# Ten of twelve pairs of merge-gate products by seven half-width products each

## The chip, the cores and the metric

The kernel runs on one core of one Trainium2 chip. Five engines matter here: TensorE (PE in the profile, its weight loads PEld), VectorE (DVE), ScalarE (ACT), GpSimd (POOL) and the DMA queues that SyncE (SP) and POOL issue to. The metric is the device time of one execution, in microseconds.

## The reference

One layer of a decoder trunk on x of 512 rows by 1024 features, all float32:

```python
h = rmsnorm(x, norm_g)
u = h @ w_in                       # split into a_x, a_z, b_q ... c_z, gate_logits
ya = pool_mixer(a_x) * silu(a_z)
yb = swa_attention(b_q, b_k, b_v, sinks) * silu(b_z)
yc = moba_attention(c_q, c_k, c_v) * silu(c_z)
ga, gb, gc = split(sigmoid(gate_logits), 3)          # each 512 x 1024
merged = ga * (ya @ w_proj_a) + gb * (yb @ w_proj_b) + gc * (yc @ w_proj_c)
out = rmsnorm(x + merged @ w_out, final_norm_g)
```

gate_logits is h (512 x 1024) times 1024 x 3072, the largest product of the layer. ya, yb and yc are 512 x 512 each.

## The kernel before

**Split precision.** Each float32 operand is kept as two float32r parts, hi (a cast on ACT, L103 for weights) and lo (value minus hi on DVE, L104). Each product is three matmuls into one PSUM bank: hi by hi, hi by lo, lo by hi (`mm3`, L125 to L128). In the trace these are the lines L126, L127, L128.

**Layout.** Activations are transposed: features on the 128 partitions, the 512 rows of x along the free axis. h is eight tiles `hT[k]` of 128 x 512, each as hi and lo. A weight block `wr` is 128 x 1024: for an output block of 128 features, the eight 128 x 128 stationary tiles of the contraction. The host packs the blocks; `weight_blocks` (L48) lists them in the order of use.

**Weights.** SP loads the raw block (`load_upto`, L91, 512 KB each, a ring of 4 buffers `wr`). `split_upto` (L106) casts it to `wh` on ACT and forms `wl` on DVE, two blocks ahead of its use (rings of 3), and then asks for the load of the fourth block ahead.

**Two stages.** Until 250.4 us of the span the input projections and the two attentions run, interleaved by a table `todo` that is keyed by matmul chunk (`at`, `tick`). The change leaves that order nearly as it was. Then comes the gate stage. It runs over the eight output blocks j of 128 features: gate a (24 matmuls of 512 columns, L534 to L543, its sigmoid on ACT), the output projection of the block before (`project_out`, L578, eight groups of three matmuls, each added to `acc` by DVE on L585), gate b, gate c, and `project` (L550): three times 12 matmuls of 512 columns, each multiplied by its sigmoid and summed on DVE (L565, L568, L569), the sum split to hi and lo (`merged[j]`). The last three blocks of w_out are left to the end, where they accumulate in PSUM (`tail_mm`, L613) while the final norm runs; its last group is cut into two of 256 columns. In every engine's queue the instructions stand in program order; a matmul waits only for its operands and its bank.

**PSUM.** Four tags of two banks: `big` (gates), `T` (projections), `S` and `PV` (output projections in this stage).

**x for the residual.** Four DMAs of 512 KB on POOL's queue (L517) fill `acc` at the start of the gate stage.

Of the kernel before, what the change touches and what calls it, by code (L numbers as in the profile page):

```python
# [46 lines left out]

def weight_blocks():  # L48

    blocks = [(u, 1024) for u in UNITS]  # L50
    late = []
    for j in range(KT):
        blocks.append((("ga", j), 1024))
        if late:
            blocks.append((("wo", late.pop()), 1024))
        blocks += [(("gb", j), 1024), (("gc", j), 1024), (("pab", j), 1024), (("pc", j), 512)]
        if j < KT - TAIL:
            late.append(j)
    blocks += [(("wo", j), 1024) for j in range(KT - TAIL, KT)]
    return blocks  # L60
# [3 lines left out]
def trunk(ctx: ExitStack, tc: tile.TileContext, a, out: bass.AP):  # L64
# [17 lines left out]
    blocks = weight_blocks()  # L82
    index = {name: n for n, (name, _) in enumerate(blocks)}
# [3 lines left out]
    def raw_tile(n):  # L87
        raw_w[n] = pool.tile([P, 1024], F32, name=f"wr{n}", tag="wr", bufs=4)
        return raw_w[n]

    def load_upto(n):  # L91
        while done["load"] <= min(n, len(blocks) - 1):
            m = done["load"]
            cols = blocks[m][1]
            nc.sync.dma_start(raw_tile(m)[:, :cols], a["w"][m][:, :cols])
# [10 lines left out]
    def split_upto(n):  # L106
        while done["split"] <= min(n, len(blocks) - 1):
# [11 lines left out]
    def split(src, name, two=None):  # L119
        hi, lo = (t2(F32R, name + "h"), t2(F32R, name + "l")) if two is None else (two[:, 0, :], two[:, 1, :])  # L120
        nc.scalar.copy(hi, src)
        nc.vector.tensor_sub(lo, src, hi.bitcast(F32))
        return hi, lo

    def mm3(ps, lh, ll, rh, rl, start, stop):  # L125
        nc.tensor.matmul(ps, lh, rh, start=start, stop=False)  # L126
        nc.tensor.matmul(ps, lh, rl, start=False, stop=False)  # L127
        nc.tensor.matmul(ps, ll, rh, start=False, stop=stop)  # L128
# [17 lines left out]
    xT = [t2(F32, f"xT{k}") for k in range(KT)]  # L146
# [10 lines left out]
    xn = pool.tile([P, NT, D], F32, name="xn", tag="v", bufs=1, padded_shape=[P, 5, 1024])  # L157
    for t in range(NT):
        nc.sync.dma_start(xn[:, t, :], a["x"][t * P:(t + 1) * P, :])
# [27 lines left out]
    for k in range(KT):  # L187
        hi, lo = t2(F32R, f"xgh{k}"), t2(F32R, f"xgl{k}")
# [57 lines left out]
    vt = []  # L246

    def evacuate(u, ps):
# [5 lines left out]
        if kind in ("cq", "ck", "bq", "bk"):  # L254
            hi, lo = split(ps, f"{kind}{i}")
            top, low = slice(0, HD), slice(HD, P)
            if kind[1] == "q":
                two = parts[u] = pair(F32R, f"{kind}{i}two")
                moves = ((two, top, 0, hi, top), (two, low, 0, lo, top),
                         (two, low, 1, hi, low), (two, top, 1, lo, low))  # L260
            else:
                his, los = parts[u] = pair(F32R, f"{kind}{i}his"), pair(F32R, f"{kind}{i}los")
# [4 lines left out]
        elif kind == "cz":  # L267
            full[u] = t2(F32, f"{kind}{i}")
# [5 lines left out]
        else:  # L274
            full[u] = t2(F32, f"{kind}{i}")
# [16 lines left out]
    def turn_v(u):  # L292
# [26 lines left out]

    def pool_mix(i):  # L320
        if not pw:
            pw_raw = t2(F32, "pw_raw")
            nc.gpsimd.dma_start(pw_raw, a["pool_w"])
            pw.extend(split(pw_raw, "pw"))
# [3 lines left out]
        full["oa", i] = t2(F32, f"oa{i}")  # L328
        nc.scalar.activation(full["oa", i], ps, AF.Copy, scale=psc_sb[:, i:i + 1])
# [10 lines left out]
    def head(s):  # L340
        if s not in heads:
# [6 lines left out]
            h.v = n if h.moba else 8 + h.par  # L348
# [43 lines left out]
    def turn(s, b):  # L392
# [19 lines left out]
        hi, lo = t2(F32R, f"pth{s}_{b}"), t2(F32R, f"ptl{s}_{b}")  # L412
# [11 lines left out]
    def weigh(s, half):  # L424
# [15 lines left out]
        if half == 1:  # L440
            kind = "oc" if h.moba else "ob"
            if h.par == 0:
                full[kind, h.block] = t2(F32, f"{kind}{h.block}")
# [19 lines left out]
    for k in range(KT):  # L463
        at(32 + 3 + 5 * k, normed, k)
        at(32 + 5 + 5 * k, normed_rest, k)
    for u in UNITS:
# [48 lines left out]
    acc = pool.tile([P, NT, D], F32, name="acc", tag="v", bufs=1, padded_shape=[P, 5, 1024])  # L515
# [239 lines left out]
```

## Time and profile before

| what | value |
|---|---|
| time, median of 3 runs | 507.12 us (506.67 to 507.14) |
| profiled execution, its own time | 506.78 us |
| its span | 505.0 us |
| mean granted TensorE clock | 0.994 |
| busy: PE / PEld / DVE / ACT / POOL | 494.8 / 402.7 / 305.1 / 232.4 / 33.3 us |
| gate stage, start to last matmul's start | 250.41 to 496.16 us |
| HBM read / written | 47.98 / 2.10 MB |

The profile is one execution. The span runs from the first to the last recorded instruction; the time of the execution is 1.78 us more. Busy times are sums of instructions; matmuls overlap one another, so the pace of TensorE is read from the starts of matmuls that follow one another, not from the length of one. PEld are weight loads, which run beside matmuls. "Idle before <- releaser" names what ended the wait of an engine.

### The profile page before, as it was taken

The page shows a single profiled execution, that of the slowest core. Times are in us where ns is not written, and L with a number is a line of the kernel's source. Part 1 is how long each engine was busy: PE and PEld are TensorE (multiplying, and loading weights), DVE is VectorE, ACT ScalarE, POOL GpSimd, SP SyncE. Part 2 cuts the span into 40 slices and gives each one's busy share as a digit, 9 for nine tenths or more (in the row PEclk, how much of TensorE's full clock was granted, in tenths as well). Part 3 has the DMA queues.
Part 4 walks back from the last instruction along what each step waited for, and adds up shares of the span by engine and source line. Part 5 has one row for each costly group of instructions (what it writes and reads, how often), then busy time and mean ns, then how long its engine had stood idle before and what let it go on. Part 6 is the DMA issues. An engine that isn't in the chain of part 4 may idle for free.

```text
span 505.0 us, 6455 instructions
## 1 busy us (share of the span) xinstructions
PE 494.8 (98%) x2297; PEld 402.7 (80%) x2297; DVE 305.1 (60%) x605; ACT 232.4 (46%) x452; POOL 33.3 (7%) x72
## 2 busy tenths in 40 slices
PE   8999999999999999999999999999999999999993
PEld 5788888888888888888888887888888888888882
DVE  5558877676788975558556626455272563433376
ACT  6655665656565675559464223132222222323344
POOL 2052000000021100000100000000000000000022
PEclk9999999999999999999999999999999999999997
DMA  8999427743622122210552231313232321313004
GB/s 258 398 257 242 147 74 179 197 125 92 174 72 104 43 83 85 83 56 29 199 182 80 85 123 64 125 65 123 85 104 85 102 85 64 125 64 125 0 2 167
DMA packets 22368, 59.94 MB, mean 119 GB/s; under 512 B 3200, under 2 KB 4224, under 8 KB 22336
## 3 DMA queue, kind: packets, MB, share of 16 engines
q1 hardware_dynamic: 21312, 56.63, 35.6%
q0 software_dynamic: 880, 2.89, 1.6%
q8 instruction: 18, 0.29, 0.2%
q14 instruction: 14, 0.11, 0.1%
q10 hardware_dynamic: 144, 0.00, 0.0%
HBM read 47.98 MB, written 2.10 MB: 99 GB/s over the span
## 4 chain that ended last, share of the span: by engine, by line
PE 95%; DVE 2%; ACT 1%; DMA 1%; issue 0%; SPq 0%; ACTq 0%
PE ps_o L438 3%; PE ps_gc L126 3%; PE ps_gb L126 3%; PE ps_gc L127 3%; PE ps_ga L128 3%; PE ps_gb L127 3%; PE ps_gc L128 3%; PE ps_gb L128 3%; PE ps_ga L127 3%; PE ps_ga L126 3%; PE ps_t L410 3%; PE ps_y L126 2%; PE ps_y L128 2%; PE ps_y L127 2%; PE ps_s L369 2%; PE ps_s L368 2%
## 5 line engine op out<-in xcount | busy, mean ns | idle before, releaser
L103 ACT CAST wh<-wr 128x1024 fp32r<-128x1024 f32 (+2 forms) x88 | 83.5, 952 | 166.5 <-PE ps_gc L127 35.7
L104 DVE TENSOR_TENSOR wl<-wr,wh 128x1024 fp32r<-128x1024 f32 (+2 forms) x84 | 91.6, 1095 | 94.1 <-ACT wh L103 93.7
L377 ACT ACTIVATE p<-p,st 128x128 f32<-128x128 f32 (+2 forms) x64 | 33.4, 523 | 34.5 <-DVE st L375 34.4
L585 DVE TENSOR_TENSOR acc<-acc,ps_y 128x512 f32<-128x512 f32 x40 | 24.8, 684 | 15.7 <-PE ps_y L128 15.7
L421 DVE TENSOR_TENSOR ptl<-ps_t,pth 128x512 fp32r<-128x512 f32 (+3 forms) x56 | 26.5, 476 | 7.3 <-ACT pth L420 6.8
L420 ACT CAST pth<-ps_t 128x512 fp32r<-128x512 f32 (+3 forms) x56 | 23.4, 418 | 12.8 <-PE ps_t L410 7.7
L128 PE MATMUL ps_ga<-hh,wl 128*128 128x512 f32 x64 | 25.3, 395 | 0.0
L127 PE MATMUL ps_ga<-hl,wh 128*128 128x512 f32 x64 | 25.3, 395 | 0.0
L128 PE MATMUL ps_gb<-hh,wl 128*128 128x512 f32 x64 | 25.3, 395 | 0.0
L126 PE MATMUL ps_gc<-hh,wh 128*128 128x512 f32 x64 | 25.3, 395 | 0.0
L127 PE MATMUL ps_gc<-hl,wh 128*128 128x512 f32 x64 | 25.3, 395 | 0.0
L128 PE MATMUL ps_gc<-hh,wl 128*128 128x512 f32 x64 | 25.3, 395 | 0.0
L126 PE MATMUL ps_gb<-hh,wh 128*128 128x512 f32 x64 | 25.3, 395 | 0.0
L127 PE MATMUL ps_gb<-hl,wh 128*128 128x512 f32 x64 | 25.3, 395 | 0.0
L126 PE MATMUL ps_ga<-hh,wh 128*128 128x512 f32 x64 | 25.3, 395 | 0.0
L637 POOL TENSOR_TENSOR yo<-acc,fg 128x512 f32<-128x512 f32 x5 | 6.4, 1294 | 241.7 <-DVE acc L627 239.4
L410 PE MATMUL ps_t<-ident,p 128*128 128x128 f32 x136 | 21.3, 272 | 0.0
L390 DVE TENSOR_SCALAR p<-p,st 128x128 f32<-128x128 f32 (+2 forms) x64 | 19.9, 358 | 0.5
L410 PEld LDWEIGHTS ps_t<-ident,p 128*128 128x128 f32 x136 | 16.7, 141 | 3.7
L438 PE MATMUL ps_o<-pth,vt 128*128 128x256 f32 (+1 forms) x64 | 17.8, 296 | 0.0
L438 PE MATMUL ps_o<-ptl,vt 128*128 128x256 f32 (+1 forms) x64 | 17.7, 300 | 0.0
L375 DVE CUSTOM_DVE_ANT_0 p<-ps_s,mask_c,nscale 128x128 f32<-128x128 f32 (+3 forms) x32 | 16.5, 545 | 1.7 <-PE ps_s L369 1.6
(390 smaller groups left out, 1263.4 us busy)
## 6 DMA issues: line engine op xcount, KB each, us to landing
wr<-in_w SPq DMA_DIRECT2D x72, 512.0 KB, 3.3
xT<-in_xT SPq DMA_DIRECT2D x8, 256.0 KB, 4.7
xn<-in_x SPq DMA_DIRECT2D x4, 512.0 KB, 8.7
wr<-in_w SPq DMA_DIRECT2D x8, 256.0 KB, 2.6
acc<-in_x POOLq DMA_DIRECT2D x4, 512.0 KB, 6.5
out<-yo SPq DMA_DIRECT2D x8, 256.0 KB, 2.3
wr<-in_w SPq DMA_DIRECT2D x8, 128.0 KB, 4.4
ck0his<-ck0h SPq DMA_DIRECT2D x4, 128.0 KB, 6.0
```

The lines of the kernel that those rows point to most:

```text
L103: nc.scalar.copy(w_hi[n][:, c], raw_w[n][:, c])
L104: (nc.gpsimd if 4 <= n < 8 else nc.vector).tensor_sub(w_lo[n][:, c], raw_w[n][:, c], w_hi[n][:, c].bitcast(F32))
L126: nc.tensor.matmul(ps, lh, rh, start=start, stop=False)
L127: nc.tensor.matmul(ps, lh, rl, start=False, stop=False)
L128: nc.tensor.matmul(ps, ll, rh, start=False, stop=stop)
L377: exps.append(nc.scalar.activation(dst, dst, AF.Exp, bias=h.st[:, i:i + 1], scale=-1.0, accum_out=h.st[:, 4 + i:5 + i]))
L390: nc.vector.tensor_scalar_mul(dst, dst, h.st[:, 12 + i:13 + i])
L410: nc.tensor.transpose(ps[:, x:x + P], h.p[:, off:off + P], ident)
L420: nc.scalar.copy(hi[:, c], ps[:, c])
L421: nc.vector.tensor_sub(lo[:, c], ps[:, c], hi[:, c].bitcast(F32))
L438: nc.tensor.matmul(h.o[:, q0:q0 + w], v, h.pt[b][e][:, x:x + w], start=n == 0 and e == 0, stop=n == 3 and e == 1)
L585: nc.vector.tensor_add(acc[:, t, c], acc[:, t, c], ps)
```

## The change

The sizes below are those of the code; none of it is a time.

- **Pairs.** The gates of one kind (a, b or c) are taken by pairs of output blocks f = 0, 1: twelve pairs. With the rows of x in halves (left, right, 256 columns each) and the contraction in halves (`hT[0..3]`, `hT[4..7]`), a pair is a 2 x 2 product of blocks. The first two pairs (a0, a1) stay as they were, 48 matmuls of 512 columns. The other ten are done by Strassen's scheme in its form with seven products (`gate_pair7`): each product is 12 matmuls of 256 columns, 84 in all.
- **Products.** In order: A by h, S13 by T3, A by h, S24 by T2, S13 by T1, D by h, S24 by h. A, S13, S24 and D are weight blocks; T1, T2, T3 are sums of h. Four of the seven accumulate in the left half of one bank `ps_ga..` (names with two letters and a number, `ps_gab2`: kind b, pair 2), so a bank holds running sums; ACT copies the running sum out to `sn` after each of the first three of them. Two products go to `ps_gd..`, one to `ps_gb..`. DVE combines (three operations of 256 columns), ACT makes the sigmoids (256, 512 and 256 columns).
- **Sums of weights.** S13 is the left halves of both blocks by a plain DMA on SP, onto which a second DMA on POOL's queue adds the second block (`accum_op`); it waits for the first. S24 is formed by two DVE additions of 512 columns in the raw tile of A, from A and S13 (L155, L156), and is then split as any block. The ring `wr` has 5 buffers, `wh` and `wl` 4.
- **Sums of h.** `sums_ready` (twice, in the first two pairs): eleven DVE operations and three ACT casts of 512 columns each time. `sums_late` after the second pair: four ACT casts and four DVE subtractions of 256 columns, into the right half of `hT[0..3]`.
- **Projections.** `project` of the pair before is put between the products: the first output block after the fourth product, the second after the sixth. They are the same 288 matmuls.
- **Output projections.** All eight blocks of w_out come after the gates. The first five accumulate in PSUM banks that the last three go on with; the 40 additions to `acc` on DVE are gone but for one. `acc` and the final norm's weights are loaded by POOL after the gates.
- **Buffers.** Most tiles of 512 columns now come from one ring of 32 units of two, `t2` has 4 in place of 31. The load of the pooling weights is issued earlier.

Core of the diff:

```diff
+DIRECT = 2
...
+def weight_items():
+    items = [(u, 1024) for u in UNITS]
+    before = []
+    for n in "abc":
+        for p in range(4):
+            if not (n == "a" and p < DIRECT):
+                a, s13, s24, d = ((("g" + n + x, p), c) for x, c in (("A", 1024), ("S13", 1024), ("S24", 1024),
+                                                                    ("D", 512)))
+                items += [a, s13, s24, *before, d]
+            else:
+                items += [(("g" + n, 2 * p + f), 1024) for f in range(2)] + before
+            before = [(("p" + n, p), 1024)]
+    items += before
+    return items + [(("wo", j), 1024) for j in range(KT)]
...
-        return pool.tile([P, S], dt, name=name, tag="t2", bufs=31)
-    def pair(dt, name):
-        return pool.tile([P, 2, S], dt, name=name, tag="two", bufs=9)
+        return pool.tile([P, S], dt, name=name, tag="t2", bufs=4)
+    def unit(dt, name, shape=(2, S)):
+        return pool.tile([P, *shape], dt, name=name, tag="u", bufs=32)
...
-        raw_w[n] = pool.tile([P, 1024], F32, name=f"wr{n}", tag="wr", bufs=4)
+        raw_w[n] = pool.tile([P, 1024], F32, name=f"wr{n}", tag="wr", bufs=5)
...
+    def load(m):
+        (kind, i), cols = items[m]
+        if kind.endswith("S24"):
+            return
+        t = raw_tile(m)
+        if kind in ("pa", "pb", "pc"):
+            r = row["pc" if kind == "pc" else "pab", 2 * i]
+            c = slice(512, 1024) if kind == "pb" else slice(0, 512)
+            nc.sync.dma_start(t.rearrange("p (b c) -> p b c", b=2),
+                              a["w"][r:r + 2, :, c].rearrange("b p c -> p b c"))
+            return
+        if kind[0] != "g" or len(kind) == 2:
+            nc.sync.dma_start(t[:, :cols], a["w"][row[kind, i]][:, :cols])
+            return
+        f1 = row[kind[:2], 2 * i]
+        if kind.endswith("A"):
+            nc.sync.dma_start(t, a["w"][f1])
+        elif kind.endswith("D"):
+            nc.sync.dma_start(t[:, :512], a["w"][f1 + 1][:, 512:])
+        else:
+            nc.sync.dma_start(t.rearrange("p (b c) -> p b c", b=2),
+                              a["w"][f1:f1 + 2, :, :512].rearrange("b p c -> p b c"))
+            nc.gpsimd.dma_start(t, a["w"][f1 + 1], accum_op=OP.add)
...
-        w_hi[n] = pool.tile([P, 1024], F32R, name=f"wh{n}", tag="wh", bufs=3)
-        w_lo[n] = pool.tile([P, 1024], F32R, name=f"wl{n}", tag="wl", bufs=3)
+        w_hi[n] = pool.tile([P, 1024], F32R, name=f"wh{n}", tag="wh", bufs=4)
+        w_lo[n] = pool.tile([P, 1024], F32R, name=f"wl{n}", tag="wl", bufs=4)
...
+            load_upto(m)
+            if items[m][0][0].endswith("S24"):
+                raw_w[m], s13 = raw_w[m - 2], raw_w[m - 1]
+                one_, two_ = slice(0, 512), slice(512, 1024)
+                nc.vector.tensor_add(raw_w[m][:, one_], raw_w[m][:, one_], s13[:, two_])
+                nc.vector.tensor_add(raw_w[m][:, two_], raw_w[m][:, two_], raw_w[m][:, one_])
             parts_of(m)
-            split_cols(m, slice(0, blocks[m][1]))
+            split_cols(m, slice(0, items[m][1]))
...
+        nc.tensor.matmul(ps, lh, rh, start=start, stop=False, skip_group_check=more)
+        nc.tensor.matmul(ps, lh, rl, start=False, stop=False, skip_group_check=more)
+        nc.tensor.matmul(ps, ll, rh, start=False, stop=stop, skip_group_check=more)
...
+    sums = {}
+    def sums_ready(i2):
+        if not sums:
+            for q in range(1, 4):
+                sums[q] = [unit(F32R, f"T{q}{x}", (4, 256)) for x in "hl"]
+        r = [unit(F32, f"r{x}{i2}") for x in (0, 1)]
+        for x in range(2):
+            for i in range(2):
+                hi, lo = hT[4 * x + 2 * i2 + i]
+                nc.vector.tensor_add(r[x][:, i, :], hi.bitcast(F32), lo.bitcast(F32))
+        b11, b12, b21, b22 = (r[x][:, :, c] for x in range(2) for c in (slice(0, 256), slice(256, 512)))
+        ta, tb, sl = t2(F32, f"ta{i2}"), t2(F32, f"tb{i2}"), slice(2 * i2, 2 * i2 + 2)
+        ta, tb = (t.rearrange("p (i c) -> p i c", i=2) for t in (ta, tb))
+        def keep(q, raw):
+            hi, lo = (t[:, sl, :] for t in sums[q])
+            nc.scalar.copy(hi, raw)
+            nc.vector.tensor_sub(lo, raw, hi.bitcast(F32))
+        nc.vector.tensor_sub(ta, b12, b22)
+        keep(3, ta)
+        nc.vector.tensor_sub(tb, b11, b12)
+        keep(1, tb)
+        nc.vector.tensor_sub(b11, ta, b11)
+        keep(2, b11)
+        nc.vector.tensor_add(b21, b21, b11)
+        sums[4, i2] = b21
...
+    def rows_part(k0, c):
+        return [(hT[k][0][:, c], hT[k][1][:, c]) for k in range(k0, k0 + 4)]
...
+    def sums_late():
+        for i in range(4):
+            hi, lo = (t[:, 256:] for t in hT[i])
+            raw = sums[4, i // 2][:, i % 2, :]
+            nc.scalar.copy(hi, raw)
+            nc.vector.tensor_sub(lo, raw, hi.bitcast(F32))
...
+    def gate_pair7(n, p, between):
+        sig, sn = unit(F32, f"sig{n}{p}"), unit(F32, f"sn{n}{p}", (4, 256))
+        left, right = slice(0, 256), slice(256, 512)
+        pa, pb, pd = bank("big", f"ps_ga{n}{p}"), bank("PV", f"ps_gb{n}{p}"), bank("S", f"ps_gd{n}{p}")
+        def product(ps, part, half, h, start):
+            wh, wl = weights(("g" + n + part, p))
+            for i in range(4):
+                c = slice(half * 512 + i * P, half * 512 + (i + 1) * P)
+                mm3(ps[:, left], wh[:, c], wl[:, c], *h[i], start and i == 0, i == 3, not start)
+            return ps[:, left]
+        def total(q):
+            return [(sums[q][0][:, i, :], sums[q][1][:, i, :]) for i in range(4)]
+        nc.scalar.copy(sn[:, 0, :], product(pa, "A", 0, rows_part(0, left), True))
+        nc.scalar.copy(sn[:, 3, :], product(pd, "S13", 0, total(3), True))
+        c11 = product(pb, "A", 1, rows_part(4, left), True)
+        nc.vector.tensor_add(sig[:, 0, left], c11, sn[:, 0, :])
+        nc.scalar.copy(sn[:, 1, :], product(pa, "S24", 0, total(2), False))
+        between(0)
+        nc.scalar.copy(sn[:, 2, :], product(pa, "S13", 1, total(1), False))
+        nc.vector.tensor_sub(sig[:, 1, right], sn[:, 3, :], sn[:, 2, :])
+        sigmoid(sig[:, 0, left], sig[:, 0, left])
+        c21 = product(pd, "D", 0, rows_part(0, right), False)
+        nc.vector.tensor_sub(sig[:, 1, left], c21, sn[:, 1, :])
+        between(1)
+        c12 = product(pa, "S24", 1, rows_part(4, right), False)
+        sigmoid(sig[:, 1, :], sig[:, 1, :])
+        sigmoid(sig[:, 0, right], c12, (n, p) == ("c", 3))
+        return sig
+    def project(n, p, sig, f):
+        wh, wl = weights(("p" + n, p))
+        if n == "a" and f == 0:
+            ms[p] = unit(F32, f"m{p}")
+        j, m = 2 * p + f, ms[p][:, f, :]
+        ps = bank("T", f"ps_p{n}{j}")
+        for i in range(4):
+            c = slice(f * 512 + i * P, f * 512 + (i + 1) * P)
+            mm3(ps, wh[:, c], wl[:, c], *y[n, i], i == 0, i == 3)
+        if n == "a":
+            nc.vector.tensor_mul(m, ps, sig[:, f, :])
+        else:
+            t = t2(F32, f"t{n}{j}")
+            nc.vector.tensor_mul(t, ps, sig[:, f, :])
+            nc.vector.tensor_add(m, m, t)
+        if n == "c":
+            merged[j] = split(m, f"mg{j}")
+    gated("a")
+    before = None
+    def between(f):
+        if before:
+            project(*before, f)
+        if before and f == 1 and before[1] == 1:
+            later = {"a": "b", "b": "c"}.get(before[0])
+            if later:
+                gated(later)
+    for n in "abc":
+        for p in range(4):
+            if n == "a" and p < DIRECT:
+                if DIRECT == 1:
+                    sums_ready(0)
+                    sums_ready(1)
+                elif p < 2:
+                    sums_ready(p)
+                sig = gate_pair(n, p)
+                if p == DIRECT - 1:
+                    sums_late()
+                between(0)
+                between(1)
+            else:
+                sig = gate_pair7(n, p, between)
+            before = (n, p, sig)
+    between(0)
+    between(1)
...
+    for j in range(KT - TAIL):
+        wo[j] = weights(("wo", j))
         for t in range(NT):
             for hf in range(2):
-                nc.vector.tensor_add(acc[:, t, c], acc[:, t, c], ps)
+                tail_mm(t, hf, [j])
```

TensorE, within pair b2 and the start of a projection (`T2h`, `T2l`: a sum of h; `wh61`: S24 of this pair; `ps_pb2`: the projection of the pair before). Before, at the end of a gate product and the start of the projection:

```order
L126 MATMUL ps_gc1_3012<-hh7_642,wh42_2928 128x512
L127 MATMUL ps_gc1_3012<-hl7_643,wh42_2928 128x512
L128 MATMUL ps_gc1_3012<-hh7_642,wl42_2929 128x512
L126 MATMUL ps_pa1_3046<-ya0h_2709,wh43_2974 128x512
L127 MATMUL ps_pa1_3046<-ya0l_2710,wh43_2974 128x512
L128 MATMUL ps_pa1_3046<-ya0h_2709,wl43_2975 128x512
```

Now:

```order
L175 MATMUL ps_gab2_3471<-T2h_2602,wh61_3476 128x256
L176 MATMUL ps_gab2_3471<-T2l_2603,wh61_3476 128x256
L177 MATMUL ps_gab2_3471<-T2h_2602,wl61_3477 128x256
L175 MATMUL ps_pb2_3551<-yb0_2960,wh62_3496 128x512
L176 MATMUL ps_pb2_3551<-yb0_2960,wh62_3496 128x512
L177 MATMUL ps_pb2_3551<-yb0_2960,wl62_3497 128x512
```

The projections are as they were, 512 columns wide; the gate's matmuls are half as wide, each with its own weight tile as before.

POOL, from the attention stage's last operation on. Before:

```order
L418 MEMSET ptl15_1_2598 128x64
L517 DMA acc_2667<-in_x 128x1024 x4
L637 TENSOR_TENSOR yo00_4280<-acc_2667,fg_2672 128x512
L637 TENSOR_TENSOR yo01_4289<-acc_2667,fg_2672 128x512
L637 TENSOR_TENSOR yo20_4323<-acc_2667,fg_2672 128x512
L637 TENSOR_TENSOR yo21_4351<-acc_2667,fg_2672 128x512
```

Now:

```order
L133 DMA wr75_3820<-in_w 128x1024
L133 DMA wr80_3982<-in_w 128x1024
L133 DMA wr85_4150<-in_w 128x1024
L726 DMA acc0_4521<-in_x 128x1024
L726 DMA acc1_4522<-in_x 128x1024
L726 DMA acc2_4523<-in_x 128x1024
L726 DMA acc3_4524<-in_x 128x1024
L729 DMA fg_4529<-in_fg 128x512 x2
```

Shown are the last three of ten accumulating loads (the S13 blocks of the ten pairs, one after another, `wr40` to `wr85`). The ten stand where the four loads of `acc` stood; `acc` and the final norm's weights follow them.

ACT and DVE at the turn from pair c1 to c2 (`wr80`: S13 of c2; `wr79`: A of c2, then S24; `wh81`, `wl81`: the parts of S24; `snc2` row L658: the copy of the first product of c2; `tc`: the projection of pair c0). Before, DVE at a like place, block j = 6:

```order
L104 TENSOR_TENSOR wl75_4061<-wr75_3929,wh75_4060 128x1024
L568 TENSOR_TENSOR tc6_4079<-ps_pc6_4066,sigc6_4021 128x512
L569 TENSOR_TENSOR m6_4023<-m6_4023,tc6_4079 128x512
L104 TENSOR_TENSOR wl76_4086<-wr76_3962,wh76_4085 128x1024
L122 TENSOR_TENSOR mg6_4082<-m6_4023,mg6_4082 128x512
L104 TENSOR_TENSOR wl77_4119<-wr77_3994,wh77_4118 128x1024
L104 TENSOR_TENSOR wl78_4151<-wr78_4028,wh78_4150 128x512
L104 TENSOR_TENSOR wl79_4184<-wr79_4064,wh79_4183 128x1024
L565 TENSOR_TENSOR m7_4182<-ps_pa7_4187,sig7_4116 128x512
```

Now, DVE and then ACT:

```order
L146 TENSOR_TENSOR wl80_4088<-wr80_3982,wh80_4087 128x1024
L668 TENSOR_TENSOR sigc1_3971<-ps_gdc1_3975,snc1_3972 128x256
L688 TENSOR_TENSOR tc1_4119<-ps_pc1_4106,sigc0_3809 128x512
L155 TENSOR_TENSOR wr79_3926<-wr79_3926,wr80_3982 128x512
L689 TENSOR_TENSOR m0_2785<-m0_2785,tc1_4119 128x512
L156 TENSOR_TENSOR wr79_3926<-wr79_3926 128x512
L170 TENSOR_TENSOR mg1_4122<-m0_2785,mg1_4122 128x512
L146 TENSOR_TENSOR wl81_4147<-wr79_3926,wh81_4146 128x1024
L146 TENSOR_TENSOR wl82_4167<-wr82_4032,wh82_4166 128x1024
```

```order
L145 CAST wh80_4087<-wr80_3982 128x1024
L613 ACTIVATE sigc1_3971<-sigc1_3971 128x512
L613 ACTIVATE sigc1_3971<-ps_gac1_3973 128x256
L169 CAST mg1_4122<-m0_2785 128x512
L658 COPY snc2_4140<-ps_gac2_4141 128x256
L145 CAST wh81_4146<-wr79_3926 128x1024
L145 CAST wh82_4166<-wr82_4032 128x1024
```

On DVE the two additions for S24 stand between the projection's operations, behind the split of S13; on ACT the cast of S24 (`wh81`) stands behind the copy of the new pair's first product.

More of the change, by code (lines that the diff above doesn't have):

```diff
@@ L45 @@
 TAIL = 3
+DIRECT = 2
 def weight_blocks():
[L50 to L60, printed above, removed]
+    names = list(UNITS)
+    for kind in ("ga", "gb", "gc", "pab", "pc", "wo"):
+        names += [(kind, j) for j in range(KT)]
+    return [(name, 512 if name[0] == "pc" else 1024) for name in names]
+def weight_items():
[12 more added lines that the diff above has]
+    return items + [(("wo", j), 1024) for j in range(KT)]
 @with_exitstack
@@ L145, in trunk @@
     nc.scalar.dma_start(g_sb, a["norm_g"])
-    xT = [t2(F32, f"xT{k}") for k in range(KT)]
+    xT = [h for k in range(0, KT, 2) for h in halves(F32, f"xT{k}")]
     for n in range(2):
@@ L257, in evacuate @@
             if kind[1] == "q":
-                two = parts[u] = pair(F32R, f"{kind}{i}two")
+                two = parts[u] = unit(F32R, f"{kind}{i}two")
                 moves = ((two, top, 0, hi, top), (two, low, 0, lo, top),
@@ L267, in evacuate @@
         elif kind == "cz":
[L268 removed]
+            kept(kind, i)
             with tc.issue_after(exps[-1].ins):
@@ L442, in weigh @@
             if h.par == 0:
-                full[kind, h.block] = t2(F32, f"{kind}{h.block}")
+                kept(kind, h.block)
             rest = t2(F32, f"rest{s}")
@@ L512, in trunk, with gated, sigmoid @@
     assert not todo, sorted(todo)
-    acc = pool.tile([P, NT, D], F32, name="acc", tag="v", bufs=1, padded_shape=[P, 5, 1024])
+    y, merged, ms = {}, {}, {}
+    def gated(n):
+        for i in range(4):
+            o, z = full["o" + n, i], full[n + "z", i]
+            nc.vector.tensor_mul(o, o, z)
+            y[n, i] = split(o, f"y{n}{i}")
+    def sigmoid(out_, in_, last=False):
+        ins = nc.scalar.activation(out_, in_, AF.Sigmoid)
+        if last:
+            with tc.issue_after(ins.ins):
+                nc.scalar.sqrt(one, one)
@@ new lines, in gate_pair @@
+    def gate_pair(n, p):
+        sig = unit(F32, f"sig{n}{p}")
+        for f in range(2):
+            wh, wl = weights(("g" + n, 2 * p + f))
+            ps = bank("big", f"ps_g{n}{p}{f}")
+            for k in range(KT):
+                c = slice(k * P, (k + 1) * P)
+                mm3(ps, wh[:, c], wl[:, c], *hT[k], k == 0, k == KT - 1)
+            sigmoid(sig[:, f, :], ps, (n, p, f) == ("c", 3, 1))
+        return sig
+    def rows_part(k0, c):
+        return [(hT[k][0][:, c], hT[k][1][:, c]) for k in range(k0, k0 + 4)]
@@ L516, in trunk @@
+    between(0)
+    between(1)
+    acc = [unit(F32, f"acc{t}", (D,)) for t in range(NT)]
     for t in range(NT):
-        nc.gpsimd.dma_start(acc[:, t, :], a["x"][t * P:(t + 1) * P, :])
-    fg_two = pair(F32, "fg")
-    fg_sb = [fg_two[:, n, :] for n in range(2)]
+        nc.gpsimd.dma_start(acc[t], a["x"][t * P:(t + 1) * P, :])
+    fg_sb = halves(F32, "fg")
     for n in range(2):
@@ L523, in trunk @@
                                               ap=[[0, P], [1, 512]]))
-    y = {}
-    def gated(n, i):
-        o, z = full["o" + n, i], full[n + "z", i]
-        nc.vector.tensor_mul(o, o, z)
-        y[n, i] = split(o, f"y{n}{i}")
-    sig_two = {}
-    def gate(n, j, sig, m):
-        wh, wl = weights(("g" + n, j))
-        ps = bank("big", f"ps_g{n}{j}")
-        for k in range(KT):
-            c = slice(k * P, (k + 1) * P)
-            mm3(ps, wh[:, c], wl[:, c], *hT[k], k == 0, k == KT - 1)
-        if m == 0:
-            sig_two[j] = pair(F32, f"sig{j}")
-        sig.append(sig_two[j][:, m, :] if m < 2 else t2(F32, f"sig{n}{j}"))
-        last_sig = nc.scalar.activation(sig[m], ps, AF.Sigmoid)
-        if (n, j) == ("c", KT - 1):
-            with tc.issue_after(last_sig.ins):
-                nc.scalar.sqrt(one, one)
@@ L607, in trunk @@
-    wo = [weights(("wo", j)) for j in last]
-    accs = {}
-    ss = const("ss", [P, 48])
+    last = list(range(KT - TAIL, KT))
+    accs, wo = {}, {}
     prod = {}
```

153 lines of the change are left out of this document (58 added, 95 removed).

## The prediction

> **What bounds the kernel now.** I read the page first, then the stages, then the starts of single matmuls. From the page, the busy times, two of the slices and the chain of waits:
>
> ```profile
> PE 494.8 (98%) x2297; PEld 402.7 (80%) x2297; DVE 305.1 (60%) x605; ACT 232.4 (46%) x452; POOL 33.3 (7%) x72
> PE   8999999999999999999999999999999999999993
> GB/s 258 398 257 242 147 74 179 197 125 92 174 72 104 43 83 85 83 56 29 199 182 80 85 123 64 125 65 123 85 104 85 102 85 64 125 64 125 0 2 167
> PE 95%; DVE 2%; ACT 1%; DMA 1%; issue 0%; SPq 0%; ACTq 0%
> ```
>
> TensorE is busy from end to end, and 95% of the chain that ends last is TensorE. The gate stage in three windows (columns: PE, PEld, DVE, ACT, POOL busy with counts, clock, DMA share, GB/s):
>
> ```profile
> 260.00:300.00 40.00, 40.00 (x173) 32.15 (x172) 19.99 (x27) 12.73 (x18) 0.00 (x0) 1.00 0.30 99
> 300.00:400.00 100.00, 100.00 (x430) 80.29 (x430) 51.01 (x67) 26.09 (x32) 0.00 (x0) 1.00 0.28 94
> 400.00:480.00 80.00, 80.00 (x345) 64.38 (x344) 33.33 (x42) 22.64 (x30) 0.00 (x0) 1.00 0.24 81
> ```
>
> TensorE has no idle time there, at clock 1.00, and its matmuls are 512 columns wide: 100/430 = 0.2326 us each. DVE is busy for half of the time, ACT for a quarter. So work taken from TensorE is time gained, as long as the other engines and the loads keep up with a shorter stage.
>
> **What a half-width matmul costs.** The end of TensorE's work already has both widths, each matmul with a weight load of its own. The starts (first column) carry the pace:
>
> ```profile
> 493.93 0.39 PE L128 MATMUL ps_z<-wh,mg 128*128 128x512 f32 x1
> 494.15 0.28 PE L126 MATMUL ps_z<-wh,mg 128*128 128x256 f32 x1
> 494.27 0.28 PE L127 MATMUL ps_z<-wl,mg 128*128 128x256 f32 x1
> ...
> 496.16 0.28 PE L128 MATMUL ps_z<-wh,mg 128*128 128x256 f32 x1
> ```
>
> ```profile
> 494.16 0.19 PEld L127 LDWEIGHTS ps_z<-wl,mg 128*128 128x128 f32 x1
> 494.28 0.19 PEld L128 LDWEIGHTS ps_z<-wh,mg 128*128 128x128 f32 x1
> ```
>
> These are 18 matmuls of 256 columns, so 2.01 us over 17 intervals: 0.1182 us each, 0.508 of 0.2326. A weight load lasts 0.19 us, longer than that interval, but the next starts 0.12 us later: loads overlap one another. So half the columns cost half the time.
>
> **The change, part by part.**
>
> *Products.* Ten pairs lose 48 matmuls of 512 columns each and gain 84 of 256: 840 x 0.1182 = 99.3 us in place of 480 x 0.2326 = 111.6 us. That is **12.3 us less**. With exactly half of 0.2326 for the narrow ones it is 97.7, so 13.9 less. The 96 matmuls of the direct pairs, the 288 of the projections and the 192 of w_out are only moved.
>
> *The period of a pair* is 84 x 0.1182 + 24 x 0.2326 = 15.51 us, laid out from its start: three products to 4.25, the fourth (S24) to 5.67, a projection to 8.46, S13 with T1 to 9.88, D to 11.30, a projection to 14.09, the last product to 15.51. What must fit into it, by these rows:
>
> ```profile
> L104 DVE TENSOR_TENSOR wl<-wr,wh 128x1024 fp32r<-128x1024 f32 x30 | 36.7, 1222 | 43.9 <-ACT wh L103 43.9
> L104 DVE TENSOR_TENSOR wl<-wr,wh 128x512 fp32r<-128x512 f32 x6 | 4.2, 692 | 22.5 <-ACT wh L103 22.5
> L585 DVE TENSOR_TENSOR acc<-acc,ps_y 128x512 f32<-128x512 f32 x32 | 19.8, 684 | 12.5 <-PE ps_y L128 12.5
> L103 ACT CAST wh<-wr 128x1024 fp32r<-128x1024 f32 x30 | 31.5, 1051 | 102.8 <-PE ps_pb L127 26.8 <-PE ps_gc L127 26.8 <-PE ps_ga L127 20.0
> L543 ACT ACTIVATE sig<-ps_ga 128x512 f32<-128x512 f32 x6 | 3.6, 594 | 0.0
> 497.76 0.40 DVE L627 TENSOR_TENSOR acc<-acc,ps_z 128x256 f32<-128x256 f32 x1
> 498.56 0.40 ACT L629 ACTIVATE sq<-acc 128x256 f32<-128x256 f32 x1
> ```
>
> DVE: four splits of 1024 columns (4.9), one of 512 (0.7), two additions for S24 (1.4), three operations of 256 (1.2), four of 512 for the projections (2.8): 11.0 us, and 12.4 where `merged` is split too. ACT: four casts of 1.05, one of 0.6, four copies and two sigmoids at 0.40, one at 0.59: 7.8 us, 9.0 with `merged`. Both fit into 15.5. The 40 additions on L585 go; they were beside TensorE, so they are no gain (32 of them 19.8 us in this window), but make room.
>
> *Sums of h.* 22 operations of 512 columns on DVE (22 x 0.69 = 15.2 us) and eight of 256 columns shared with ACT. They start when the attention stage lets DVE go (about 248) and are first needed at 250.4 + 27.9 + 1.4 = 279.7, after the direct pairs and their projections. With `ya`, six splits and the S24 additions I count 30 us of DVE work up to the first S24 product (282.5), in 34 us. Hidden, cost 0; 3.5 us of cover are left.
>
> *Loads.* A pair loads 2.25 MiB (2.36 MB) in 15.5 us, 152 GB/s, against 94 in the window above; the first slices moved 242 to 398. The new thing is the accumulating DMA, which before's trace does not have. Its nearest rows (issue and landing of `acc`, the same 512 KB on the same queue, and the plain loads):
>
> ```profile
> L517 POOL DMA_DIRECT2D acc<-in_x x4: 540/544/554, 247.4 to 249.0; - x4
> DMA to landing us min/median/max: 4.4/6.5/7.6
> wr<-in_w SPq DMA_DIRECT2D x72, 512.0 KB, 3.3
> ```
>
> Below, it takes 4.4 (a load alone); above, twice that, 8.8, since it reads and writes its destination. I take 6.5, the median of the row it is nearest to. What it may take: S13 of the next pair uses the buffer of this one's S13. That comes free with the first addition for S24 on DVE (L155), which stands behind the cast of S13 (from 11.30, once D's end has freed a `wh`), its split and L668: 11.30 + 1.05 + 1.22 + 0.40 + 0.69 = 14.7. Then SP's load (3.3), two hand-offs (0.3), then POOL's. The cast of the new S13 comes at 26.8. So 26.8 - 14.7 - 3.6 = **8.5 us** are free; 7.8 in the three pairs where a projection's operation stands ahead of L155. TensorE itself is late only 3.3 us after that (it needs S13 at 32.4, a cast and a split later). At 6.5 the cost is 0, at 8.8 it is 9 x 8.8 - 6 x 8.5 - 3 x 7.8 - 3.3 = 1.5 us. Behind SP's waiting load stand the pair's projection weights and D, which are needed later than S13; behind POOL's wait only the next accumulate.
>
> *S24.* A new chain: L155, L156, cast, split, all after S13 lands. It ends at about 18.4 where 19.76 is needed. In the last pairs of kind c it is tight: L156 ends at 16.8, but the cast on ACT stands behind the copy of the new pair's first product (ends 16.93 + 0.40), so cast 18.4, split 19.6, against 19.76. A hand-off here is short:
>
> ```profile
> 267.18 1.05 ACT L103 CAST wh<-wr 128x1024 fp32r<-128x1024 f32 x1 [4.43 <-PE ps_gc L127]
> 268.26 1.22 DVE L104 TENSOR_TENSOR wl<-wr,wh 128x1024 fp32r<-128x1024 f32 x1 [5.29 <-ACT wh L103]
> ```
>
> The cast ends at 268.23 and the split starts 0.03 later. I put 0.5 us each for the two tight pairs and 0.5 for the start of the first pair of seven products: 1.5 us, bounds 0 and 5 (0.5 in each of ten pairs).
>
> *Rest.* The output projections in one piece at the end take 5.6 us a block, each with one split: covered. The end behind TensorE is as before. The tighter rings move some casts in the attention stage, all of work that is needed microseconds later: 0.
>
> **The sum.** 506.78 - 12.3 + 1.5 = 496.0 for an execution like the profiled one; the median shown is 0.34 higher. I predict **496.2 us**.
>
> **Rivals.**
>
> 1. *The accumulating loads set the period (slower).* The place is the buffer loop above: cost 9L - 77.7 for a landing of L us. From L = 10.0 the whole gain is gone. If it passes the data three times (source, destination read, destination write), 4.4 + 3.3 + 3.3 = 11.0: 21.3 us lost on 507.1 - 12.3: **516 us**. For it: nobody reads a destination in before's trace, and the queue's landings already spread to 7.6. Against: those 7.6 were four loads queued within 1.6 us; here one comes every 15.5 us.
> 2. *A part of each matmul does not shrink with its columns (slower).* If weight loads did not overlap one another, a narrow matmul would take 0.19: 840 x 0.19 = 159.6 against 111.6, 48 us more than before: **555 us**. For it: PEld is busy 80% of the span. Against: the 18 starts 0.118 apart. The Trainium skill, "TensorE: Matmul & The Clock Gate", section "Back-to-back issue gap", gives such a part: in a stream of weight loads and matmuls about 81 ns at 128 columns and 131 at 512, so some 98 at 256 by interpolation (an estimate), three quarters of the wide one. By that the ten pairs would take 840 x 0.75 x 0.2326 = 146.5, 35 us more. The trace does not agree: 0.118 against 0.2326.
> 3. *S24 comes late in every pair.* If DVE is one split and one operation of 512 columns behind (1.9 us), pairs with 1.4 us of slack lose 0.5, the others 1.8: seven and three make 8.9 less the 1.5 already counted, so 496.2 + 7.4: **about 504 us**. For it: DVE is at 71 to 80% of the period, in strict order. Against: the tally leaves it 3 us a pair.
> 4. *The sums of h are late* by up to 4 us, once: **about 500**.
>
> **Chances.** Forecast 0.57, rival 1 0.17 (0.12 of it past the point where it is slower, 0.02 level), rival 2 0.04, rival 3 0.17, rival 4 0.05. About 0.2% is what can be told from no change here. Faster 0.57 + 0.17 + 0.05 + 0.03 = 0.82, level 0.02, slower 0.12 + 0.04 = 0.16. The forecast alone is 493 to 500 (13.9 gained and nothing lost, to 12.3 gained and 5 lost). The range must take in rivals 3, 4 and the milder part of 1: 492.5 to 506.
>
> **What would show it.** Right: starts of `ps_ga..` matmuls of 256 columns 0.118 apart; 15.5 us from pair to pair; TensorE busy through the stage; landings of the accumulates under 8.5. Wrong by rival 1: TensorE idle before the S13 product, released by `wl` of S13, and casts that wait for POOL's DMA. By rival 2: 256-column starts 0.17 apart or more with no idle time. By rival 3: short waits before `ps_ga..` with S24's `wl`, each pair. By rival 4: one wait at about 280 to 283.

## The result and the profile after

| | before | after |
|---|---|---|
| median of 6 runs each | 507.13 us | 503.18 us |
| ratio, 95% interval | 1 | 0.9921 (0.9900 to 0.9941) |
| profiled execution / its span | 506.78 / 505.0 us | 502.68 / 500.8 us |

The kernel is faster by 3.95 us. I had forecast 10.9, to 496.2. The measured time lies in the range, on the side of rival 1 (the mild part) and next to the 504 of rival 3. The time alone does not tell which of them is the cause.

From the page of the changed kernel, the busy times, then two windows of the gate stage (columns as before), then what TensorE waited for (us in total, times, longest):

```profile
PE 483.8 (97%) x2657; PEld 412.1 (82%) x2657; DVE 334.8 (67%) x658; ACT 264.3 (53%) x528; POOL 42.0 (8%) x82
```

```profile
300.00:400.00 100.00, 95.29 (x655) 87.25 (x654) 61.04 (x84) 44.19 (x76) 5.21 (x6) 1.00 0.55 144
400.00:480.00 80.00, 78.12 (x434) 66.91 (x433) 42.67 (x56) 30.26 (x46) 4.13 (x7) 1.00 0.41 132
```

```profile
PE ps_gab L175 <- ACT snb L658: 3.6, 4, 1.2
PE ps_gac L177 <- DVE wl L146: 1.5, 2, 0.8
...
PE ps_gac L175 <- ACT snc L658: 1.1, 2, 0.9
```

TensorE now has idle time where it had none: 4.7 us of 100 in one window, 1.9 of 80 in the other. All of it stands ahead of or inside one product of each pair of kinds b and c, S24 by T2. Elsewhere the narrow matmuls follow one another 0.117 to 0.12 us apart. So the narrow matmul is as cheap as forecast, and what is missing is lost in waits.

What they wait for shows in one pair, b1. The SP and POOL queues first, then ACT, DVE and TensorE (start, duration):

```profile
310.61 0.38 SPq L131 DMA_DIRECT2D wr<-in_w  x1
327.41 0.38 SPq L131 DMA_DIRECT2D wr<-in_w  x1
330.91 0.38 SPq L118 DMA_DIRECT2D wr<-in_w  x1
332.04 0.34 SPq L128 DMA_DIRECT2D wr<-in_w  x1
332.98 0.34 SPq L126 DMA_DIRECT2D wr<-in_w  x1
344.24 0.38 SPq L131 DMA_DIRECT2D wr<-in_w  x1
```

```profile
331.86 0.87 POOL L133 DMA_DIRECT2D wr<-in_w  x1 [15.35 <-ACT wh L145]
```

```profile
324.10 1.05 ACT L145 CAST wh<-wr 128x1024 fp32r<-128x1024 f32 x1 [2.85 <-DMA wr<-in_w]
...
328.57 2.00 ACT L145 CAST wh<-wr 128x1024 fp32r<-128x1024 f32 x2 [0.89 <-DVE wr L156]
330.47 0.37 ACT L658 COPY snb<-ps_gab 128x256 f32<-128x256 f32 x1
...
340.93 1.05 ACT L145 CAST wh<-wr 128x1024 fp32r<-128x1024 f32 x1 [2.87 <-DMA wr<-in_w]
```

```profile
325.18 1.23 DVE L146 TENSOR_TENSOR wl<-wr,wh 128x1024 fp32r<-128x1024 f32 x1 [2.61 <-ACT wh L145]
326.32 0.42 DVE L668 TENSOR_TENSOR sigb<-ps_gdb,snb 128x256 f32<-128x256 f32 x1
326.66 0.68 DVE L155 TENSOR_TENSOR wr<-wr,wr 128x512 f32<-128x512 f32 x1
...
343.49 0.68 DVE L155 TENSOR_TENSOR wr<-wr,wr 128x512 f32<-128x512 f32 x1
```

```profile
329.49 0.28 PE L177 MATMUL ps_gbb<-h,wl 128*128 128x256 f32 x1
330.89 0.38 PE L175 MATMUL ps_gab<-T2h,wh 128*128 128x256 f32 x1 [1.13 <-ACT snb L658]
```

Read it as a ring. L155 at 326.66 is the last reader of S13's buffer. SP loads the next S13 into it at 327.41; POOL's accumulate goes out at 331.86; the cast of that S13, at 340.93, waited 2.87 us for the DMA; L155 follows at 343.49. One turn: 0.75 + 4.45 + 9.07 + 2.56 = **16.83 us**, where TensorE needs 15.4 for a pair of output blocks (worked out below). From 294.37 to 409.97 seven turns took 16.5 on average.

The end of the chain is the same ring seen from TensorE. S13's cast late at 324.10 makes L155 and L156 late, so the casts of S24 and of the projection weights (328.57) are late, and the copy of the new pair's first product (330.47 to 330.84) stands behind them on ACT. That copy must leave the bank before S24's product can go on in it. The row names the copy; the cause lies several steps up.

The landing of the ten accumulating loads (from the start of the issue), first over all, then for the second alone (issued at 273.87), which had one plain load beside it (P, issued at 275.23):

```profile
DMA to landing us min/median/max: 5.2/8.4/8.9
DMA to landing us min/median/max: 5.2/5.2/5.2
```

### The profile page after: what moved, and what is told of

Its sections match the earlier page's. It is cut to its first block, busy times and chain, and to the rows that moved or that the text cites. A ratio compares the mean times of both kernels' runs of the same rounds, so it can differ in the third digit from the quotient of the medians.

```text
span 500.8 us, 7371 instructions
## 1 busy us (share of the span) xinstructions
PE 483.8 (97%) x2657; PEld 412.1 (82%) x2657; DVE 334.8 (67%) x658; ACT 264.3 (53%) x528; POOL 42.0 (8%) x82
## 4 chain that ended last, share of the span: by engine, by line
PE 93%; DVE 2%; ACT 2%; DMA 1%; issue 1%; SPq 0%; ACTq 0%; DVEq 0%
PE ps_o L493 3%; PE ps_t L465 3%; PE ps_z L177 2%; PE ps_z L176 2%; PE ps_z L175 2%; PE ps_s L424 2%; PE ps_gab L175 2%; PE ps_s L423 2%; PE ps_gac L177 2%; PE ps_gac L175 2%; PE acc_az L175 2%; PE acc_bz L175 2%; PE acc_bq L175 2%; PE acc_ax L175 2%; PE acc_cz L175 1%; PE acc_v L175 1%
## 5 line engine op out<-in xcount | busy, mean ns | idle before, releaser
L146 DVE TENSOR_TENSOR wl<-wr,wh 128x1024 fp32r<-128x1024 f32 (+2 forms) x100 | 111.0, 1120 | 64.8 <-ACT wh L145 64.4
L145 ACT CAST wh<-wr 128x1024 fp32r<-128x1024 f32 (+2 forms) x104 | 98.7, 960 | 102.2 <-issue 35.8
L475 ACT CAST pt<-ps_t 128x512 fp32r<-128x512 f32 (+3 forms) x56 | 23.3, 418 | 13.9 <-PE ps_t L465 7.9
L476 DVE TENSOR_TENSOR pt<-ps_t,pt 128x512 fp32r<-128x512 f32 (+3 forms) x56 | 26.5, 475 | 5.2 <-ACT pt L475 4.8
L177 PE MATMUL ps_z<-wh,mg 128*128 128x512 f32 (+1 forms) x67 | 25.8, 385 | 0.0
L176 PE MATMUL ps_z<-wl,mg 128*128 128x512 f32 (+1 forms) x67 | 25.8, 385 | 0.0
L175 PE MATMUL ps_z<-wh,mg 128*128 128x512 f32 (+1 forms) x67 | 25.8, 385 | 0.0
L133 POOL DMA_DIRECT2D wr<-in_w x10 | 8.7, 873 | 201.9 <-ACT wh L145 77.7
L430 DVE CUSTOM_DVE_ANT_0 p<-ps_s,mask_s,nsink 128x256 f32<-128x256 f32 (+1 forms) x32 | 13.9, 445 | 2.3 <-PE ps_s L424 1.9
L175 PEld LDWEIGHTS ps_z<-wh,mg 128*128 128x128 f32 x67 | 12.6, 188 | 2.8
L177 PEld LDWEIGHTS ps_z<-wh,mg 128*128 128x128 f32 x67 | 12.6, 188 | 2.8
L501 DVE TENSOR_TENSOR ob<-ps_o,rest 64x512 f32<-64x512 f32 x8 | 5.5, 683 | 12.4 <-ACT rest L500 12.3
L175 PE MATMUL acc_bq<-h,wh 128*128 128x512 f32 x32 | 13.4, 418 | 0.0
L175 PE MATMUL acc_ax<-h,wh 128*128 128x512 f32 x32 | 13.3, 415 | 0.0
```

Source lines behind the costliest of these rows:

```text
L145: nc.scalar.copy(w_hi[n][:, c], raw_w[n][:, c])
L146: (nc.gpsimd if 4 <= n < 8 else nc.vector).tensor_sub(w_lo[n][:, c], raw_w[n][:, c], w_hi[n][:, c].bitcast(F32))
L175: nc.tensor.matmul(ps, lh, rh, start=start, stop=False, skip_group_check=more)
L176: nc.tensor.matmul(ps, lh, rl, start=False, stop=False, skip_group_check=more)
L177: nc.tensor.matmul(ps, ll, rh, start=False, stop=stop, skip_group_check=more)
L430: nc.vector.tensor_tensor_reduce(out=dst, in0=ps[:, :n], in1=mask, scale=scale, scalar=least, op0=OP.add, op1=OP.min, accum_out=h.st[:, i: ...
```

## Experiments: is it the ring of S13's buffer?

Theory: the ring sets the period. Rivals: S24's chain on DVE and ACT is too long in itself; or the DMA engines are too busy.

**The two loads swapped.** S13 of a pair is asked for ahead of A. Then D's buffer, free 11 us earlier, takes it, and A, which had been loaded some 20 us ahead of its use, takes the one that L155 frees.

```diff
+    swapped = {}
+    for m, ((kind, _), _) in enumerate(items):
+        if kind.endswith("S13"):
+            swapped[m - 1], swapped[m] = m, m - 1
...
-            load(done["load"])
+            load(swapped.get(done["load"], done["load"]))
```

> Only the order of two loads is changed: S13 of a pair is asked for ahead of A, so it takes the buffer that D of the pair before sets free, not the one of the S13 before it. Theory (the buffer loop: in the changed kernel the S13 loads go out 16.8 us apart, 0.75 for the addition L155, 4.45 to the start of the accumulate, 9.07 to the cast, 2.56 to the next L155): the loop is gone, the waits of ACT's cast for POOL's DMA go, and with them the 0.8 to 1.3 us ahead of the S24 product in the pairs of kind b: 495.5 to 497.5. What stays is up to 1 us in each pair of kind c. Rival (S24's own chain of additions, cast and split is too long in every pair, whenever S13 lands): 502 to 504, the same waits ahead of the S24 product. Rival (the accumulates take the DMA engines, so that something else lands late now): 499 to 502, with waits for A or D.

Measured **493.39 us**, ratio to before 0.9726 (0.9711 to 0.9742): 9.8 us faster than the changed kernel with the same instructions, the same bytes and the same additions, and below the expected band. Its window, and the landing of its accumulates in the stage:

```profile
300.00:400.00 100.00, 100.00 (x695) 92.52 (x694) 65.62 (x91) 49.14 (x82) 6.08 (x7) 1.00 0.60 155
```

```profile
DMA to landing us min/median/max: 5.2/5.4/7.1
```

TensorE has no idle time. The tight places in the last pairs of kind c are gone too, so they had been the ring's doing as well. DMA carries more per second than in the changed kernel (155 against 144 GB/s), so its engines had room. The landing fell from 8.4 to 5.4 without a change to the load itself: it now goes out (320.71 for one) when A, P and D, issued at 309.14, 312.64 and 313.78, have landed (the last at 317.2).

**The second load without adding** (the sum of the two blocks is left out), and **without the second load** (left out too).

```diff
-            nc.gpsimd.dma_start(t, a["w"][f1 + 1], accum_op=OP.add)
+            nc.gpsimd.dma_start(t, a["w"][f1 + 1])
```

> The second load of S13 is made without adding (it overwrites), on the same queue, with the same wait; the sum of the two blocks is left out. Theory (loop, and adding is what makes that load long): landing 5.5 to 6.5 in place of 8.2 to 8.9, a loop of 14 to 15 us, under the 15.5 of a pair: 495.5 to 498. Rival (the landing is long because three other loads are in flight beside it, not because it adds): landing stays above 8, 502 to 503.5. Rival (S24's chain): landing shorter, time 502 to 504.

> The second load of S13 is left out altogether, and so the sum of the two blocks; all else as in the changed kernel. Theory (loop): 0.75 + 4.4 + 2.6 is far below 15.5, so no wait ahead of S24 in kind b: 495 to 497. Rival (S24's chain by itself): 502 to 504. What is left between this run and 494.8 is what the S24 chain costs without any question of landing.

Measured 493.81 (0.9729, 0.9711 to 0.9748) and 493.28 us (0.9721, 0.9706 to 0.9735), both some 1.7 us below their bands. Landing of the load without adding, at the old place with the same three loads beside it:

```profile
DMA to landing us min/median/max: 6.1/6.7/7.2
```

The median is just above the 5.5 to 6.5 that I expected. So adding makes some 1.7 of the 8.4, and the loads beside it some 3 (8.4 against 5.4 with the loads swapped). The software queue's share of the 16 engines, with adding (the changed kernel), without adding, and with no second load:

```profile
q0 software_dynamic: 2320, 8.13, 7.6%
```

```profile
q0 software_dynamic: 2320, 8.13, 4.8%
```

```profile
q0 software_dynamic: 880, 2.89, 1.7%
```

Ten loads take 3.1% of the engines' span plain and 5.9% adding: adding costs about twice the engine time. With no second load at all the time is that of the swapped loads (493.28 against 493.39). So once it is out of the ring, making S13 by an accumulating load costs nothing that can be measured.

**A shorter ring, loads in the old order.** The first addition for S24 is put ahead of the split of S13, where it lies beside S13's cast on ACT.

```diff
+            one_, two_ = slice(0, 512), slice(512, 1024)
+            if items[m][0][0].endswith("S13"):
+                nc.vector.tensor_add(raw_w[m - 1][:, one_], raw_w[m - 1][:, one_], raw_w[m][:, two_])
             if items[m][0][0].endswith("S24"):
                 raw_w[m], s13 = raw_w[m - 2], raw_w[m - 1]
-                one_, two_ = slice(0, 512), slice(512, 1024)
-                nc.vector.tensor_add(raw_w[m][:, one_], raw_w[m][:, one_], s13[:, two_])
```

> The changed kernel with its loads in their old order (S13 still waits for the buffer of the S13 before it); only the first addition for S24 on DVE (L155) is put ahead of the split of S13 and of L668, where it lies beside the cast of S13. The buffer is then free when the split ends, some 1.0 us earlier in each turn of the loop. Theory (the loop of 16.8 us is what costs, microsecond by microsecond, above the 15.4 of a pair): loop 15.7 to 15.9, so 494 to 497, with little or no waiting ahead of S24 in kind b. Rival (what the swap and the runs without adding gained was room on the DMA engines, not a shorter loop): landings stay at 8.2 to 8.9 and the time stays at 501 to 504.

Measured **493.50 us** (0.9726, 0.9710 to 0.9742), just under the band. Landings and turns of the ring:

```profile
DMA to landing us min/median/max: 8.2/8.4/9.1
```

```profile
308.56 0.38 SPq L131 DMA_DIRECT2D wr<-in_w  x1
324.06 0.38 SPq L131 DMA_DIRECT2D wr<-in_w  x1
339.11 0.38 SPq L131 DMA_DIRECT2D wr<-in_w  x1
354.96 0.38 SPq L131 DMA_DIRECT2D wr<-in_w  x1
```

This run tells the ring from busy engines. The landings are as long as in the changed kernel, 8.4; the turns are 15.5, 15.1 and 15.9 in place of 16.8; and the whole 9.7 us is back. Long landings cost nothing as long as the ring fits into the pair. One microsecond of order on DVE was worth 9.7, since it is paid in every turn.

**A longer ring, and the same delay outside it.** Two more additions of 512 columns, whose result nobody reads, ahead of L155: once in the changed kernel, once with the loads swapped.

```diff
+                for q in range(2):
+                    nc.vector.tensor_add(t2(F32, f"idle{m}{q}"), raw_w[m][:, one_], s13[:, two_])
                 nc.vector.tensor_add(raw_w[m][:, one_], raw_w[m][:, one_], s13[:, two_])
```

> The changed kernel with two more additions of 512 columns on DVE (1.2 us, into a tile that nobody reads) ahead of L155; on DVE a projection's operation now also stands ahead of it. All other work and all loads as in the changed kernel. Theory (the buffer loop sets the period): the loop grows by 1.2 to 1.9 us in each of eight turns: 511 to 519. Rival (DVE has room, 29% of the period, and the loss came from busy DMA engines): 502 to 506.

> The same two additions in the run with the two loads swapped, where S13 does not wait for L155. They delay S24's own chain, and A's load, by 1.2 to 1.9 us. Theory: the loop is gone, so no 1.2 a pair; where S24's chain has less slack than that (1.4 us by the tally in kind b, 0.15 in the last pairs of kind c), short waits: 493.5 to 497. Rival (any delay on DVE in this place costs its length in every pair): 505 to 510.

Measured **525.15 us** (1.0355, 1.0306 to 1.0403) and **497.66 us** (0.9810, 0.9795 to 0.9824). Both are above their bands. In the ring, the delay costs 22.0 us; outside it, the same delay costs 4.3. In the first, seven turns from 296.78 to 430.53 took 19.1 us on average, 2.6 more than in the changed kernel, not the 1.2 to 1.9 that I gave. One turn shows what else stands there: from the split of S13 at 349.52, both operations of a projection (L690 at 351.00 and L691 at 352.20) stand ahead of L155's addition, beside the two added ones. That addition starts at 353.52, 2.5 us after L690; in the turn of the changed kernel shown above it follows L668 at once. In the second run, the delay takes up the slack of S24's chain: in the last six pairs the first matmul of the next projection waits, and in the last two also S24's product, 0.2 to 0.5 us each time.

Two things beside the delay differ in these runs. In both, two matmuls of the next projection stand among those of S24's product on TensorE. And in the run in the ring TensorE's granted clock is lower, 0.984 to 0.987 against 0.994 to 0.997 in the run outside it. The same window of the two, the clock third from the end:

```profile
300.00:400.00 100.00, 87.71 (x569) 79.13 (x568) 58.76 (x84) 38.76 (x67) 5.20 (x6) 0.97 0.49 126
300.00:400.00 100.00, 99.24 (x686) 91.29 (x685) 70.75 (x99) 47.99 (x80) 5.33 (x7) 1.00 0.56 151
```

Seven turns 2.6 us longer make 18 of the 22.0 us; what part the clock has in them is not separated. So the mechanism of rival 3 exists, and 1.2 us of extra work on DVE brings it out; in the changed kernel it does not act by itself.

**The moves without the products.** All twelve pairs direct; order, weaving, output projections and buffers as in the changed kernel.

```diff
-            if not (n == "a" and p < DIRECT):
+            if False:
...
-            if n == "a" and p < DIRECT:
-                if DIRECT == 1:
...
+            if True:
                 sig = gate_pair(n, p)
-                if p == DIRECT - 1:
-                    sums_late()
```

> All twelve pairs are done directly, 48 matmuls of 512 columns each; no products of sums, no sums of h or of weights, no accumulating loads. The rest of the change stays (order of the gates by kind, projections behind the next pair, all of w_out at the end, buffers, other loads). Theory (these moves cost nothing and gain nothing, as TensorE was busy from end to end): 506.3 to 507.8. Rival (the moves themselves gain or cost): outside that range, and then the products are worth more or less than the difference of the two kernels.

Measured 507.47 us (1.0002, 0.9992 to 1.0011), as expected: the new order, the tighter buffers and the 40 additions taken from DVE neither gain nor cost. What the products alone are worth is therefore read against before: 507.17 - 493.39 = **13.8 us**.

**The cover of the sums of h.** With the loads swapped, only one direct pair; then also with the sums begun in the last two blocks of the attention stage.

```diff
-DIRECT = 2
+DIRECT = 1
```

> As the run with the two loads swapped (493.4), but only the first pair is direct and eleven are done by seven products, with all sums of h in the first pair's time. TensorE has 48 x 0.2326 - 84 x 0.1165 = 1.4 us less to do. The point is the sums: they have one direct pair (11.2 us) of cover in place of two and their projections (27.9). If DVE needs the 30 us counted for the sums, the splits and the rest, the first S24 product waits 5 to 8 us and the time is 497 to 500. If the sums are much shorter than counted, no wait and 492.

> As the run before this one, one direct pair and swapped loads, but the sums of h are begun in the last two blocks of the attention stage. Where DVE has the room there (72% busy from 100 to 250 us), the wait of the first products shrinks to 0 to 3 us: 492 to 495. If the sums push the attention's own operations on DVE, TensorE waits ahead of the gate stage instead: 495 to 499.

Measured 492.31 (0.9706, 0.9690 to 0.9723) and 492.34 us (0.9707, 0.9692 to 0.9721). The first is not the 497 to 500 that I expected with a wait, but the 492 that I gave for sums much shorter than counted: one direct pair is cover enough. In the run with the loads swapped and two direct pairs, DVE's sums run from 249.95 to 272.2, and the first product that reads T3 starts 8 us later:

```profile
249.95 2.50 DVE L521 TENSOR_TENSOR r<-h 128x512 f32<-128x512 f32 x4
...
271.76 0.41 DVE L643 TENSOR_TENSOR h<-r,h 128x256 fp32r<-128x256 f32 x1
```

```profile
280.43 0.28 PE L179 MATMUL ps_gda<-T3h,wh 128*128 128x256 f32 x1
280.55 0.28 PE L180 MATMUL ps_gda<-T3l,wh 128*128 128x256 f32 x1
...
281.25 0.28 PE L180 MATMUL ps_gda<-T3l,wh 128*128 128x256 f32 x1
```

How the run with one direct pair hides the rest is open. These two are the fastest kernels here, 15.0 us under before.

## Why the prediction was right and wrong

**What bounded the kernel, and the pace: right, a little mis-sized.** The gain of the products is 13.8 us where I put 12.3 (and 13.9 for exactly half). With the loads swapped, S13's loads keep time with the pairs:

```profile
315.54 0.37 SPq L135 DMA_DIRECT2D wr<-in_w  x1
...
392.54 0.37 SPq L135 DMA_DIRECT2D wr<-in_w  x1
```

Five pairs in 77.00 us are 15.40 each, so a narrow matmul takes (15.40 - 24 x 0.2326) / 84 = 0.117, not 0.1182; in the rows above it is (281.25 - 280.43) / 7 = 0.117. Rival 2 is out. The Trainium skill, "TensorE: Matmul & The Clock Gate", section "Back-to-back issue gap", has about 81 ns at 128 columns and 131 at 512, by which a narrow one would take three quarters of a wide one (an estimate); no run here shows that.

**What was taken to be hidden: right.** Sums of h, output projections at the end, tighter rings: all at 0. The run with all pairs direct shows it for the moves and the rings, the run with one direct pair for the sums of h.

**The step that failed: the cost of S13's buffer loop, put at 0.** The mechanism, the buffer and the formula were written down, as rival 1; two sizes fed into it were too small:

- the landing of the accumulate: 6.5 taken, 8.8 as the upper bound; measured 8.2 to 8.9 in the stage, and 9.07 from issue to the cast in the turn shown;
- the load and its hand-offs: 3.6 taken (the median of before's loads, 3.3, and 0.3); measured 4.45.

The rest of the turn, from the cast of S13 to SP's next load, was right: 3.36 taken, 2.56 + 0.75 = 3.31 measured. With both sizes as in the turn shown, 9L - 77.7 for L = 9.07 + 0.85 gives 11.6 us; the mean turn was 16.5, not 16.83. The difference to the run with the loads swapped is 9.8. So the forecast was 12.3 gained and 1.5 lost, and it came out as 13.8 gained and 9.8 lost.

In the two profiles the loss stands in the gate stage: from the first gate matmul to the last matmul of all it takes 241.84 us (250.20 to 492.04) in the changed kernel, and 232.32 (251.03 to 483.35) with the loads swapped. The idle time of TensorE makes only 6.6 us of these 9.5, since a wait costs more between the starts of matmuls than the profile calls idle (at 329.49 to 330.89: 1.40 less the usual 0.117, where 1.13 is idle). From start to start the ten waits make 8.2; the other 1.3 are matmuls in between that start a little further apart.

The sign that I gave for rival 1 was wrong too: TensorE idle ahead of S13's product. That product does not wait. S24's does, since its chain hangs on S13 and has less slack (1.4 us by my tally, where S13's product had 3.3).

I took the median landing of a row (6.5) that came from four loads queued together, and argued that here one comes alone every 15.5 us. It does not come alone: the rows of SP show P, D and A going out within 2 us of it. I had written that P and D stand behind SP's waiting load, but not that they then go out together with the accumulate. The same event, L155 and the splits behind it, frees the buffers of S13, A, P and D one after another, so the four loads are bunched by the ring itself. Those three and the accumulate are 1.8 MB; at the 242 to 398 GB/s that I had quoted they take 5 to 8 us (an estimate), and the accumulate goes out in their midst. That could have been worked out before.

**S24's chain (1.5 us taken): not needed.** The runs with the loads swapped and with no second load show no wait there, the pairs of kind c included. Rival 3 gave the right time, 504, for a wrong reason: its waits are where it said, ahead of S24's product, but they vanish when only loads are reordered.

**The choice of the likeliest case** thus went wrong by this one ring: I gave 0.17 to it, with only 0.03 for a mild one that is still faster than before. The sum without it was 494.8; the runs without it gave 493.3 to 493.8.

## What to carry to other kernels

When a buffer is filled, read and refilled once in a period, add up the whole turn (last reader, load, second load, cast, split, back to the last reader) with the hand-offs, and compare it with the period; a turn over it is paid every time, and time taken out of the turn comes back just as often. Before giving such a ring another buffer, look for a tile that is loaded far ahead of its use: swapping two loads gave 9.8 us here, and moving one addition gave 9.7. And price a transfer by what is in flight beside it, above all by what the same event sets free.

## What the runs showed of the hardware

An accumulating DMA of 512 KB on POOL's queue takes 0.87 us to issue (0.54 without adding). From the start of the issue it lands in 5.2 us with one plain load beside it (the second of the changed kernel), and in 8.2 to 8.9 with three. In the same two places without adding it lands in 3.7 and in 6.1 to 7.2, so adding makes some 1.5 to 1.7 us. It takes about twice the engine time of a plain one (5.9% against 3.1% of the engines' span for ten). The Trainium skill, "DMA: Bandwidth & Descriptors", section "Anatomy of one DMA — SWDGE (gpsimd) path", has a fit of 2.0 us and 1 us for each 436 KB, which makes 3.2 for this size (an estimate). The shortest plain load of this size on that queue took 3.5 (one of `acc`, in the run with the sums begun early), which is near it; every adding one took 5.1 or more.
